# The eight column-tiled products of a modulation part issued as one group, once its four weight tiles have landed

## The chip, the core and the metric

The kernel runs on one core of a Trainium2 chip. The metric is the device time of one execution in microseconds (us). TensorE (PE) multiplies; PEld is its weight load, which overlaps the products; VectorE (DVE), ScalarE (ACT) and GpSimd (POOL) do elementwise work; SP issues most of the transfers from memory.

## What is computed

The reference is a network of four layers over 256 latent and 256 context tokens of 1024 features. Layer i mixes tokens by i % 3 (0: gated DeltaNet, 1: differential attention, 2: mLSTM), so layers 0 and 3 are DeltaNet layers; a dense squared-ReLU MLP follows. Each of the two sub-layers is modulated by vectors that come from the conditioning, six per layer and stream:

```
m_lat = jnp.split((s_lat @ w_mod[i] + b_mod[i])[:, None, :], 6, axis=-1)
m_ctx = jnp.split(s_ctx @ w_mod[i] + b_mod[i], 6, axis=-1)
hl = modulate(xl, m_lat[0], m_lat[1])          # x * (1 + scale) + shift
...
xl = layer_norm(ALPHA * xl + m_lat[2] * yl, ln_g[i, 0], ln_b[i, 0])
xl = layer_norm(ALPHA * xl + m_lat[5] * sq_relu_mlp(modulate(xl, m_lat[3], m_lat[4]), w1[i], w2[i]), ...)
```

`w_mod[i]` is 1024 by 6144. Only two rows are multiplied by it (context and latent conditioning), so the weights are the moving operand and the two rows the stationary one.

## The kernel before

Dense products (`dense`, lines 165 to 175; `passes`, line 218) take blocks of 128 output features. A weight block is loaded by SP (`load`, line 143), split into two parts of reduced width by ACT (`whi`, line 161) and DVE (`wlo`, line 162), and multiplied in three passes by eight k-tiles: 24 products of 128 by 512.

The modulation of a layer is cut into 12 parts of 512 columns. A part has four weight tiles of 512 KB (tag `wm`, four buffers, `WM`, so one part fills them all), each with two k-tiles side by side. `mod_chunk` (line 353) multiplies a part: for each of its four tiles, two products whose stationary operand is 128 by 32 (`sil`, a window that puts the two conditioning rows at one of four pairs of columns). Each product writes to 32 of the 128 partitions of one PSUM bank (`tile_position`), so tile g uses column groups 0 and 1 of the array where g is even, 2 and 3 where it is odd. In the trace one product is two instructions: a tile is 4, a part is 16. Four parts gather in one bank (`modps`); then ACT copies it (`modsb`, line 369) and `mod_cols` (line 372) turns it into columns.

The first four parts of layer 0 belong to `proj_start` (line 224), where the order on PE is written out by hand. The other 44 wait in `self.todo` (layer 0 has four parts of its own vectors first, the order is by layer and part). `fill` (line 678) takes the next: it asks for its four tiles on the SP queue and calls `mod_chunk`. The mixers call it between dense blocks, at places that constants give: `MODS` for the DeltaNet layers (line 43), `AM` for attention, `MM` for mLSTM; `run` (line 646) does what is left over at the end of a mixer. So layer 0 does 20 parts, the layers after it 8 each.

The order in the code is not yet the order on the engines. The program is built in a Tile context with `schedule_with_timeline_sim=True`: a planner simulates the engines and transfers and issues on each engine what its simulation has ready, earlier code first; `high_priority(offset=n)` moves what stands in its block ahead, `issue_after(i)` lets it come after instruction i on that engine, and a manual dependency adds an edge, with a semaphore (`Sync`) or for the order alone (`NoSync`). A tile of a pool waits until one of the tag's buffers is free. On the chip every engine runs the planned order; an instruction that waits holds up what is behind it on its engine or queue.

Before the change the eight products of a part are bound to nothing but their own tile, so the planner issues each tile's pair as soon as it reckons that tile to be there, and puts other products in between.

Of the kernel before, what the change touches and what calls it, by code (L numbers as in the profile page):

```python
# [17 lines left out]
P = 128  # L18
# [22 lines left out]
MODTAG = "oos"  # L41
AHEAD = 1
# [31 lines left out]
# columns of the packed per-partition parameters  # L74
# [7 lines left out]
# columns of the packed shape-only constants  # L82
# [8 lines left out]
# diagonal blocks of the triangular inverse: (partition quarter, half, direction, block)  # L91
# [20 lines left out]
class Net:  # L112
# [52 lines left out]
    def dense(self, w, act, ps, streams=BOTH):  # L165
        """ps[out feature, token] = sum over the eight k-tiles, in three exact float32r passes"""
# [3 lines left out]
        for k in range(8):  # L170
# [4 lines left out]
            nc.tensor.matmul(ps[:, c], lo[:, s], rh[:, c], start=False, stop=k == 7)  # L175
# [7 lines left out]
    def heads(self, kind, j):  # L183
        """the first blocks of a mixer"""
# [3 lines left out]
    def prepare_first(self, srcs, early=WHL):  # L188
        """blocks of the next stage, in parts while the norm before it runs"""
        self.ahead = [self.wblock(s, keep=i >= early, tag=AW) for i, s in enumerate(srcs)]  # L190

    def proj_first(self, srcs, act, streams=BOTH):
        """blocks at the start of a stage: their context halves, then their latent halves, k-tile by k-tile"""
# [24 lines left out]
    def passes(self, w, act, ps, k, c):  # L218
        """one k-tile's part of a block's product"""
        for i, (lhs, rhs) in enumerate(((w[0], act[k][0]), (w[0], act[k][1]), (w[1], act[k][0]))):  # L220
            self.nc.tensor.matmul(ps[:, c], lhs[:, c128(k)], rhs[:, c], start=k == 0 and i == 0, stop=k == 7 and i == 2)  # L221
            yield

    def proj_start(self, srcs, act):
        """the first blocks of all, as their operand comes in by quarters (q): M its modulation, C the operand, U a block's part"""
# [53 lines left out]
    def new_act(self, nm, n=8):  # L279
        """k-tiles of an operand as (hi, lo)"""  # L280
# [6 lines left out]
    def new_h(self):  # L287
        """k-tiles of a sub-layer's operand as (hi, lo), then the same in pairs"""
# [4 lines left out]
    def setup(self):  # L293
# [9 lines left out]
        # a window of 32 columns puts the two streams at any of the first four pairs of columns  # L303
# [18 lines left out]
        # the normalized rows come as -2 n  # L322
# [7 lines left out]
        self.mod = {}  # L330
        self.hn = 0
# [7 lines left out]
    def later(self, n, f, *a):  # L339
        """emit f(*a) after n further blocks"""  # L340
# [12 lines left out]
    def mod_chunk(self, li, q, u, n, ws, gs=range(4)):  # L353
# [1385 lines left out]
```

## Time and profile before

| what | value |
|---|---|
| runs | 2792.53, 2791.49, 2788.17 us, median 2791.49 |
| profiled execution | span 2787.1 us from the first to the last instruction; its time outside the span is not listed |
| PE | 2648.8 us busy (95%) |
| PEld | 2121.4 us (76%) |
| DVE | 1569.6 us (56%) |
| ACT | 1282.5 us (46%) |
| transfers | 379.75 MB, mean 136 GB/s |

Times of the trace are us from the start of the span. Busy is the union of an engine's instructions. An instruction of PE is drawn with a modelled end, so two neighbours can overlap. "Idle before" is the time in which the engine had nothing to do just before the instruction, with what released it.

### The profile page before, as it was taken

Reading aid. Unit: us, or ns where it says so; the run is one execution under the profiler, and the core shown is the slowest. Engines: PE = TensorE matmul, PEld = TensorE weight load, DVE = VectorE, ACT = ScalarE, POOL = GpSimd, SP = SyncE. Lnnn points to the kernel's source line nnn. Section 1 sums busy time; section 2 is a strip of 40 time slices with the busy share of each in tenths; the row PEclk is TensorE's granted clock in tenths of the full one; section 3 lists DMA queues with packets and bytes.
Section 4 is the critical chain, followed back from the end, with each engine's and each line's share of the span. In section 5 each row is a group of like instructions: output and inputs, shape, how many; then the busy total and the mean of one; then the engine's idle time right before and its main releaser. Section 6 shows DMA issues by size and latency. Waiting matters only on the chain. (4 is left out here: it accounts for less than half of the span.)

```text
span 2787.1 us, 40628 instructions
## 1 busy us (share of the span) xinstructions
PE 2648.8 (95%) x15984; PEld 2121.4 (76%) x15984; DVE 1569.6 (56%) x3353; ACT 1282.5 (46%) x2504; POOL 105.2 (4%) x172
## 2 busy tenths in 40 slices
PE   8999999999999999899999999999999998988998
PEld 4766578888888655888888876688888886678997
DVE  4688756533347455653334644563333679877555
ACT  4545376533344344353334434452333465546554
POOL 0111011000000000000000000000000011011000
PEclk9999999999999999999999999999999989889999
DMA  7587754132232334313233234423232246534353
GB/s 306 187 290 251 249 165 154 46 99 93 97 117 84 107 127 159 106 53 99 91 98 120 82 127 173 171 70 98 91 98 91 91 149 242 187 114 137 121 184 127
DMA packets 105982, 379.75 MB, mean 136 GB/s; under 512 B 12120, under 2 KB 14168, under 8 KB 105792
## 3 DMA queue, kind: packets, MB, share of 16 engines
q1 hardware_dynamic: 91808, 328.24, 34.7%
q0 software_dynamic: 13696, 48.06, 5.2%
q8 instruction: 125, 2.05, 0.3%
q10 hardware_dynamic: 288, 0.87, 0.1%
q14 instruction: 65, 0.53, 0.1%
HBM read 353.97 MB, written 23.15 MB: 135 GB/s over the span
## 5 line engine op out<-in xcount | busy, mean ns | idle before, releaser
L161 ACT CAST whi<-raw 128x1024 fp32r<-128x1024 f32 x360 | 377.3, 1049 | 845.7 <-PE psd L174 781.2
L162 DVE TENSOR_TENSOR wlo<-raw,whi 128x1024 fp32r<-128x1024 f32 x360 | 440.5, 1224 | 425.7 <-ACT whi L161 423.7
L173 PE MATMUL psd<-hh,whi 128*128 128x512 f32 (+1 forms) x1552 | 581.9, 375 | 4.2 <-ACT whi L161 4.1
L175 PE MATMUL psd<-hh,wlo 128*128 128x512 f32 (+1 forms) x1552 | 579.1, 373 | 0.7 <-DVE wlo L162 0.5
L174 PE MATMUL psd<-hl,whi 128*128 128x512 f32 (+1 forms) x1552 | 579.2, 373 | 0.0
L173 PEld LDWEIGHTS psd<-hh,whi 128*128 128x128 f32 x1552 | 293.5, 189 | 82.4 <-issue 19.1
L175 PEld LDWEIGHTS psd<-hh,wlo 128*128 128x128 f32 x1552 | 293.4, 189 | 71.6 <-issue 17.1
L174 PEld LDWEIGHTS psd<-hl,whi 128*128 128x128 f32 x1552 | 293.7, 189 | 65.6 <-issue 16.3
L173 PE MATMUL psd<-u,whi 128*128 128x512 f32 (+1 forms) x928 | 337.4, 364 | 1.2 <-ACT whi L161 1.2
L175 PE MATMUL psd<-u,wlo 128*128 128x512 f32 (+1 forms) x928 | 337.6, 364 | 0.1
L174 PE MATMUL psd<-u,whi 128*128 128x512 f32 (+1 forms) x928 | 337.5, 364 | 0.0
L546 DVE SCALAR_TENSOR_TENSOR xa<-psd,mod,xa 128x256 f32<-128x256 f32 x280 | 126.5, 480 | 306.9 <-PE psd L175 276.1
L173 PEld LDWEIGHTS psd<-u,whi 128*128 128x128 f32 x928 | 175.2, 189 | 31.4 <-ACT whi L161 1.6
L174 PEld LDWEIGHTS psd<-u,whi 128*128 128x128 f32 x928 | 175.1, 189 | 30.1
L175 PEld LDWEIGHTS psd<-u,wlo 128*128 128x128 f32 x928 | 175.2, 189 | 29.9 <-DVE wlo L162 0.3
L364 PE MATMUL modps<-wm,sil 128*32 128x512 f32 x768 | 167.0, 627 | 14.0 <-DVE sil L306 7.0
L277 DVE TENSOR_TENSOR u<-relu,u 128x512 fp32r<-128x512 f32 (+1 forms) x128 | 79.7, 625 | 64.8 <-ACT u L276 64.8
L788 DVE SCALAR_TENSOR_TENSOR kq<-conv,convh,kq 128x508 f32<-128x508 f32 (+3 forms) x128 | 85.5, 687 | 2.6 <-ACT kq L781 2.2
L364 PEld LDWEIGHTS modps<-wm,sil 128*32 128x32 f32 x768 | 25.9, 110 | 74.8 <-issue 46.8
L221 PE MATMUL psd<-hh,khi 128*128 128x256 f32 (+1 forms) x248 | 73.3, 303 | 3.5 <-ACT hh L430 3.5
L221 PE MATMUL psd<-hl,khi 128*128 128x256 f32 (+1 forms) x248 | 76.2, 308 | 0.1
L629 ACT ACTIVATE relu<-relu 128x512 f32<-128x512 f32 (+1 forms) x128 | 73.4, 579 | 3.6
(390 smaller groups left out, 4359.3 us busy)
## 6 DMA issues: line engine op xcount, KB each, us to landing
raw<-in_w_dram SPq DMA_DIRECT2D x256, 512.0 KB, 3.5
wm<-in_w_mod_dram SPq DMA_DIRECT2D x192, 512.0 KB, 5.4
raw<-in_w_in_a_dram SPq DMA_DIRECT2D x61, 512.0 KB, 4.9
raw<-in_w_qkog_c_dram SPq DMA_DIRECT2D x17, 512.0 KB, 4.7
row<-gcd POOLq DMA_DIRECT2D x16, 512.0 KB, 5.0
raw<-in_w_out_a_dram SPq DMA_DIRECT2D x16, 512.0 KB, 4.3
raw<-in_w_qk_b_dram SPq DMA_DIRECT2D x16, 512.0 KB, 4.3
ed<-row SPq DMA_DIRECT2D x12, 512.0 KB, 3.8
```

The source lines that it names most:

```text
L161: nc.scalar.copy(hi, raw)
L162: nc.vector.tensor_tensor(out=lo, in0=raw, in1=hi.bitcast(F32), op=ALU.subtract)
L173: nc.tensor.matmul(ps[:, c], hi[:, s], rh[:, c], start=k == 0, stop=False)
L174: nc.tensor.matmul(ps[:, c], hi[:, s], rl[:, c], start=False, stop=False)
L175: nc.tensor.matmul(ps[:, c], lo[:, s], rh[:, c], start=False, stop=k == 7)
L221: self.nc.tensor.matmul(ps[:, c], lhs[:, c128(k)], rhs[:, c], start=k == 0 and i == 0, stop=k == 7 and i == 2)
L277: self.nc.vector.tensor_tensor(out=lo, in0=src, in1=hi.bitcast(F32), op=ALU.subtract)
L364: nc.tensor.matmul(self.mps[r:r + 32, :], self.sil[:, 2 * g + i, 6 - 2 * u:38 - 2 * u], ws[g][:, 512 * i:512 * i + 512], start=u == 0 and ...
L546: i = getattr(self.nc.vector, name)(**k).ins
L629: nc.scalar.activation(r, r, AF.Square)
L788: nc.vector.scalar_tensor_tensor(out=y3[:, :, o], in0=x3[:, :, i], scalar=tap(t), in1=y3[:, :, o], op0=ALU.mult, op1=ALU.add)
```

## The change

`mod_chunk` gets the list of its tiles' loads. The first of its eight products then depends on all four loads, and each further one follows the one before it in issue order. `fill` puts the group behind the last dense product that was written before it (`self.mm`, kept by `dense` and `passes`) and gives it a priority of 1000 (`MPRI`). The loads move to `fetch_mod`: those of the next part are asked for right behind the group of the part before, except behind the last part of a layer's share (`QUOTA`), where the next `fill` asks for its own. Comments were removed, too.

```diff
+MPRI = 1000
+QUOTA = 20, 8, 8, 8
...
-            nc.tensor.matmul(ps[:, c], lo[:, s], rh[:, c], start=False, stop=k == 7)
+            self.mm = nc.tensor.matmul(ps[:, c], lo[:, s], rh[:, c], start=False, stop=k == 7).ins
...
+    def depend(self, i, on, wait=False):
+        self.tc.add_manual_dep(i, on.name, mybir.DependencyInfo(mybir.DependencyClass.Sync if wait else mybir.DependencyClass.NoSync,
+                                                                mybir.DependencyReason.DATA), reason="depend")
-    def mod_chunk(self, li, q, u, n, ws, gs=range(4)):
+    def mod_chunk(self, li, q, u, n, ws, gs=range(4), loads=()):
...
+        for l in loads:
+            self.depend(mm[0], l, True)
+        for a, b in zip(mm, mm[1:]) if loads else ():
+            self.depend(b, a)
...
+            self.quota = QUOTA[n]
...
-        for li, q in self.todo[:n]:
+        for _ in range(min(n, len(self.todo))):
             self.tick()
-            ws = []
-            for g in range(4):
-                ws.append(self.wp.tile([P, 1024], F32, tag="wm", name="wm", bufs=WM))
-                self.load(ws[-1], self.ins["w_mod"][li, q, g])
-            sb = self.mod_chunk(li, q, q % 4, 4, ws)
+            self.fetch_mod()
+            li, q = self.todo.pop(0)
+            ws, loads = self.fetched
+            self.fetched = None
+            with self.tc.issue_after(self.mm), self.tc.high_priority(offset=MPRI):
+                sb = self.mod_chunk(li, q, q % 4, 4, ws, loads=loads)
...
-        self.todo = self.todo[n:]
+            self.quota -= 1
+            if self.quota:
+                self.fetch_mod()
+
+    def fetch_mod(self):
+        if self.fetched is None and self.todo:
+            l, q = self.todo[0]
+            ws = [self.wp.tile([P, 1024], F32, tag="wm", name="wm", bufs=WM) for _ in range(4)]
+            self.fetched = ws, [self.load(w, self.ins["w_mod"][l, q, g]) for g, w in enumerate(ws)]
```

## Rows read from the trace of the kernel before

**Rows 1.** Page, busy us (share of the span) and instructions of two engines.
```profile
PE 2648.8 (95%) x15984; PEld 2121.4 (76%) x15984; DVE 1569.6 (56%) x3353; ACT 1282.5 (46%) x2504; POOL 105.2 (4%) x172
```

**Rows 2.** Page, costliest groups: count, busy us, mean ns, idle before and its releaser.
```profile
L364 PE MATMUL modps<-wm,sil 128*32 128x512 f32 x768 | 167.0, 627 | 14.0 <-DVE sil L306 7.0
```

**Rows 3.** Timeline of PE, 164.8 to 167.2 us: start, us, instruction, count.
```profile
165.01 0.39 PE L174 MATMUL psd<-hl,whi 128*128 128x512 f32 x1
165.24 0.39 PE L175 MATMUL psd<-hh,wlo 128*128 128x512 f32 x1
165.56 1.05 PE L364 MATMUL modps<-wm,sil 128*32 128x512 f32 x4
166.54 0.50 PE L173 MATMUL psd<-hh,whi 128*128 128x512 f32 x1
```

**Rows 4.** Timeline of PE, 252 to 256 us.
```profile
252.92 1.92 PE L364 MATMUL modps<-wm,sil 128*32 128x512 f32 x16
254.78 0.50 PE L173 MATMUL psd<-hh,whi 128*128 128x512 f32 x1
255.11 0.40 PE L174 MATMUL psd<-hl,whi 128*128 128x512 f32 x1
```

**Rows 5.** Timeline of PE, first and last piece of the 117 after the start.
```profile
54.87 1.90 PE L364 MATMUL modps<-wm,sil 128*32 128x512 f32 x10
...
2430.18 1.05 PE L364 MATMUL modps<-wm,sil 128*32 128x512 f32 x4
```

**Rows 6.** Five stages, line 364 alone: PE busy us (instructions), granted clock, DMA share, GB/s.
```profile
54.00:331.00 277.00, 54.46 (x256) 1.00 0.70 244
331.00:375.00 44.00, 17.10 (x64) 0.88 0.72 250
923.00:1094.00 171.00, 26.60 (x128) 1.00 0.41 141
1623.00:1778.00 155.00, 25.88 (x128) 1.00 0.49 175
2300.00:2432.00 132.00, 25.48 (x128) 0.92 0.62 215
```

**Rows 7.** The same stages, all work: PE, PEld, DVE, ACT, POOL busy, granted clock, DMA.
```profile
54.00:331.00 277.00, 270.04 (x1744) 182.60 (x1742) 220.79 (x513) 135.84 (x264) 27.31 (x42) 1.00 0.70 244
331.00:375.00 44.00, 35.29 (x582) 19.00 (x582) 17.84 (x31) 16.73 (x42) 1.83 (x4) 0.88 0.72 250
923.00:1094.00 171.00, 168.60 (x763) 103.72 (x762) 85.93 (x227) 70.47 (x190) 0.00 (x0) 1.00 0.41 141
1623.00:1778.00 155.00, 155.00 (x688) 105.46 (x686) 74.96 (x242) 64.86 (x154) 3.98 (x6) 1.00 0.49 175
2300.00:2432.00 132.00, 114.45 (x1051) 80.67 (x1051) 116.69 (x279) 75.10 (x156) 10.52 (x13) 0.92 0.62 215
```

**Rows 8.** Loads of `wm` issued from 1676.9 to 1678.6 us, one part.
```profile
L146 SPq DMA_DIRECT2D wm<-in_w_mod_dram x4: 328/401/422, 1676.9 to 1678.3; - x4
...
DMA to landing us min/median/max: 3.5/5.2/6.6
```

**Rows 9.** Timeline of PE, first and last products of that part.
```profile
1683.90 1.05 PE L364 MATMUL modps<-wm,sil 128*32 128x512 f32 x4
...
1693.96 1.05 PE L364 MATMUL modps<-wm,sil 128*32 128x512 f32 x4
```

**Rows 10.** Timeline of PE, 362 to 372 us, with the idle time before in brackets.
```profile
367.33 1.92 PE L364 MATMUL modps<-wm,sil 128*32 128x512 f32 x4 [2.30 <-DMA wm<-in_w_mod_dram]
```

**Rows 11.** Line 364 on PE from 54 to 375 us: idle before, us and times.
```profile
  DMA wm<-in_w_mod_dram: 3.2, 2
```

**Rows 12.** Waits of the SP queue: us in total, times, longest.
```profile
SPq L146 <- PE modps L364: 334.0, 100, 15.7
```

**Rows 13.** Waits of all engines, longest total: us, times, longest.
```profile
ACT whi L161 <- PE psd L174: 781.2, 278, 11.1
```

More of the change, by code (lines that the diff above doesn't have):

```diff
@@ L220, in passes @@
         for i, (lhs, rhs) in enumerate(((w[0], act[k][0]), (w[0], act[k][1]), (w[1], act[k][0]))):
-            self.nc.tensor.matmul(ps[:, c], lhs[:, c128(k)], rhs[:, c], start=k == 0 and i == 0, stop=k == 7 and i == 2)
+            self.mm = self.nc.tensor.matmul(ps[:, c], lhs[:, c128(k)], rhs[:, c], start=k == 0 and i == 0, stop=k == 7 and i == 2).ins
             yield
@@ L359, in mod_chunk @@
             self.mps = self.ps("modps", self.mod_tag)
+        mm = []
         for g in gs:
@@ L363, in mod_chunk @@
                 r = 32 * (2 * (g % 2) + i)
-                nc.tensor.matmul(self.mps[r:r + 32, :], self.sil[:, 2 * g + i, 6 - 2 * u:38 - 2 * u],
-                                 ws[g][:, 512 * i:512 * i + 512], start=u == 0 and g < 2, stop=u == n - 1 and g >= 2,
-                                 tile_position=(0, r))
+                mm.append(nc.tensor.matmul(self.mps[r:r + 32, :], self.sil[:, 2 * g + i, 6 - 2 * u:38 - 2 * u],
+                                           ws[g][:, 512 * i:512 * i + 512], start=u == 0 and g < 2, stop=u == n - 1 and g >= 2,
+                                           tile_position=(0, r)).ins)
+        for l in loads:
+            self.depend(mm[0], l, True)
+        for a, b in zip(mm, mm[1:]) if loads else ():
+            self.depend(b, a)
         if u == n - 1 and gs[-1] == 3:
@@ L678, in fill @@
     def fill(self, n=1):
-        for li, q in self.todo[:n]:
+        for _ in range(min(n, len(self.todo))):
             self.tick()
-            ws = []
-            for g in range(4):
-                ws.append(self.wp.tile([P, 1024], F32, tag="wm", name="wm", bufs=WM))
-                self.load(ws[-1], self.ins["w_mod"][li, q, g])
-            sb = self.mod_chunk(li, q, q % 4, 4, ws)
+            self.fetch_mod()
+            li, q = self.todo.pop(0)
+            ws, loads = self.fetched
+            self.fetched = None
+            with self.tc.issue_after(self.mm), self.tc.high_priority(offset=MPRI):
+                sb = self.mod_chunk(li, q, q % 4, 4, ws, loads=loads)
             if q % 4 == 3:
                 self.later(1, self.mod_cols, li, sb, range(q - 3, q + 1))
-        self.todo = self.todo[n:]
+            self.quota -= 1
[6 more added lines that the diff above has]
+            self.fetched = ws, [self.load(w, self.ins["w_mod"][l, q, g]) for g, w in enumerate(ws)]
     def weave(self, n, dense, *gens):
```

## The prediction, made before the change was run

> **What bounds the kernel now.** I read the page's busy times first. TensorE (PE) is busy for 95% of the span, VectorE (DVE) for 56% [rows 1]: in the whole, time taken off PE should come off the span. A busy share is a mean, though, so I then asked which PE work the change touches. The modulation products (`modps`, line 364) hold PE for 167.0 us [rows 2]. These are 192 weight tiles of four instructions each; 16 of the tiles belong to the start, which the change leaves alone, so 176 tiles, or 44 parts, remain.
>
> The timeline of PE then shows why these products cost what they do. In a stream of dense products one starts every 0.23 us, although each is drawn 0.39 us long. A modulation tile on its own (four instructions, two of the four column groups of the array) is drawn 1.05 us, keeps the next product away for 0.98 us, and starts 0.32 us after its forerunner instead of 0.23 [rows 3]. When all four tiles of a part stand together, sixteen instructions are drawn 1.92 us, the next product starts 1.86 us after the first of them, and is itself followed after 0.33 us instead of 0.23 [rows 4]. So four tiles apart cost 3.92 us between starts and four together 1.86. Between the first and the last piece after the start [rows 5] I counted 117 unbroken pieces in the timeline for the 44 parts; the rest of the working is what happens when they become 44.
>
> Last I cut the span into the stages in which the pieces lie, first with line 364 alone [rows 6], then with every engine [rows 7]. The reader is to see that the five stages differ: PE is full in the first, third and fourth; in the second and fifth it stands idle for 9 of 44 and 18 of 132 us, while DVE is busy for 117 of the 132.
>
> **The change, part by part.**
>
> *Eight products together.* No instruction is added or removed on PE; the pieces merge. From the stage table, minus parts times 1.92: 54.46 - 16 x 1.92 = 23.7; 17.10 - 4 x 1.92 = 9.4; 26.60 - 8 x 1.92 = 11.2; 25.88 - 15.36 = 10.5; 25.48 - 15.36 = 10.1 [rows 4, 6]. Sum 65.0 us. The seams come on top. One seam costs 0.09 us before the piece, gives 0.07 back where the next product starts before the drawn end, and costs 0.10 behind: 0.12 us [rows 3, 4]. The stages hold 46, 11, 20, 20 and 20 pieces, so 30, 7, 12, 12 and 12 seams go: 3.6, 0.8, 1.4, 1.4, 1.4. Together PE gets free for 27.3, 10.3, 12.7, 12.0 and 11.6 us: 73.9 us.
>
> *How much of that reaches the end.* This is where I choose. In the third and fourth stage PE is idle for 2.4 and 0 us and DVE is at half, so nothing else is near: I take 90% and 95%, 11.4 and 11.4. In the first stage PE is full, but DVE is busy for 220.8 of 277 us, which becomes 88% of the shorter stage: convolutions, splits and the triangular inverse will sometimes be late next. I take three quarters, 20.5. In the second stage PE already has gaps that the pieces partly fill: half, 5. In the fifth DVE is as busy as PE and the inverse sets the pace of the middle: 45%, 5.2 [rows 7]. Sum 53.5 us. The bounds of this term are 0 and 73.9.
>
> *The wait.* The first product of a part now waits for four transfers, where each tile's first product waited for its own; behind it on PE stand all dense products and transposes, and for those wait the evacuations on ScalarE (ACT) and DVE. The four tiles of one part, asked for back to back, landed 3.5 to 6.6 us after their issue [rows 8]. The planner used the first of them at 1683.90 and the last at 1693.96, 9.1 us after the last landing (1678.3 + 6.6) [rows 8, 9]: it reckons loads later than they come, so a group put after the last one has cover. Against that stands the end of the first layer, where products waited 2.30 us for their tile [rows 10]. Bounds: a gain of 3.2 us, all that PE waited for modulation tiles in the first two stages [rows 11], and a loss of 44 x 3.1 us = 136 us if PE stands each time from the first landing to the fourth. I take 0, since of the two rows the first is that of a part with dense work around it, as nearly all are.
>
> What a wait costs beyond itself: after the 2.30 us the four instructions took 1.92 us and not 1.05 [rows 10], half speed, and the stage's granted clock was 0.88 [rows 7]. The Trainium skill, page "TensorE: Matmul & The Clock Gate", Part 1, says that the throttled state is the default and that activity releases it. The row agrees. By the rule each wait would also double the group behind it, 1.92 us more, 44 x 1.92 = 84 us on top of the loss bound; by the rows of the dense stages, which kept a clock of 1.00, nothing is added.
>
> *The loads move.* They are asked for one part ahead. On the SP queue each part issues the same four loads; the queue stood 334.0 us waiting for modulation products to release their buffers, and the weight blocks' loads go through the same queue [rows 12]. Before, a buffer was refilled as its own tile was done; now four come free within 1.9 us and refill in a burst. A part's cycle becomes at least 1.9 + 6.6 = 8.5 us. The first stage has 277/16 = 17 us for a part, the second 44/4 = 11, the others 16 to 21. So only the second can run late, and its cover is the recurrence, which leaves PE idle there; without this cover up to a few us per part would show, which is in my half. Of the POOL queue nothing is moved. The weight blocks are covered as well: ACT's casts wait for PE 781.2 us in all, not for loads [rows 13].
>
> *Priority.* The group and ACT's copy of the bank go ahead of other ready work: each pushes others back by 1.9 us on PE, work that must be done anyway. Cost 0, by PE being in order and full; the upper bound is one group before each step of a chain, in the fifth stage 8 x 1.9 = 15 us, which is in the 45%.
>
> **Sum.** The profiled span is 2787.1 us, the median of the runs 2791.5, 4.4 more. 2787.1 - 53.5 = 2733.6 for such a span, **2738 us** for the median.
>
> **The rivals.**
>
> *All of it pays.* DVE's 88% is still under PE's share, so the first and fifth stage may shrink in full and the 3.2 us of waits go too: 2791.5 - 73.9 - 3.2 = 2714. Against it: the idle PE in the second and fifth stage.
>
> *Other engines take over in the two DeltaNet layers.* If the chains of DVE and ACT set the first, second and fifth stage, only 11.4 + 11.4 us remain: 2768. For it: DVE's 117 of 132 us in the fifth. Against: no idle PE in the first. The Trainium skill, page "Trainium Kernel Development and Optimization", Performance Expectations, holds matmul busy time to be a bad metric and the weight loads' busy share a good one. That share is 66% in the first stage (182.6 of 277), so by the rule PE is less full there than its row says. The 0.23 us between starts under 0.39 us drawn agree that drawn times overlap, and this is why I cost by starts.
>
> *The wait for four takes the place of the pieces: slower.* If the planner's loads are early against the chip's in the new order, PE stands in front of each group with everything queued behind. It decides from a mean stand of 73.9/44 = 1.7 us per part; with 3.1 us each it is 2791.5 - 73.9 + 136 = 2854. For it: the 2.30 us. Against: the 9 us of cover.
>
> *It does not do what it says.* The order is planned anew, and other products could still get between the eight, or the planner could have to hold groups back for a bank: 2791.
>
> **How the numbers follow.** Chances: forecast 0.50 (2725 to 2755), all of it 0.17, other engines 0.20, the wait 0.09, nothing 0.04. A measurement of this kernel tells about 0.2% (5.6 us) from no change. Faster by more than that are the first three: 0.87; within it the last: 0.04; slower: 0.09. The range runs from 2713, the full price, to 2776, which takes in the case of the other engines with some us of new planning noise; the wait, the nothing and a little of the spread stay outside.
>
> **What would show it.** Right: 44 pieces of sixteen in PE's timeline after the start, each some 1.92 us; line 364 busy for 167 - 65 = 102 us; PE's idle time nearly unchanged in the third and fourth stage, each 11 us shorter; DVE's share in the first near 88%. Wrong: pieces of four still there; an idle time of PE ended by the modulation's loads above some 20 us; the stages to the end of each mixer unchanged with more idle PE, ended by DVE; a granted clock below 1.00 in the first stage.

## The result, and the profile after

The changed kernel takes **2750.53 us** (median of four runs, 2748.84 to 2754.96), the kernel before beside it 2789.83: a ratio of 0.986 with a 95% interval of 0.9847 to 0.9873, 39.3 us less. The forecast was 2738: the direction and the main cause held, and the time came out 12.5 us above it. Two further sets of runs of the same order of instructions gave 0.9866 (0.9846 to 0.9887) and 0.9871 (0.9854 to 0.9888), 34 to 37 us against the runs beside them, so the effect is some 34 to 39 us.

First the page of the changed kernel: busy time per engine, then the group of the modulation products with its count, busy us, mean ns, and idle time before them.

```profile
PE 2589.6 (94%) x15984; PEld 2126.0 (77%) x15984; DVE 1567.0 (57%) x3353; ACT 1282.2 (47%) x2504; POOL 103.3 (4%) x172
...
L373 PE MATMUL modps<-wm,sil 128*32 128x512 f32 x768 | 106.7, 640 | 23.1 <-DMA wm<-in_w_mod_dram 15.8
```

Beside [rows 1, 2]: the instructions are as many as before, the modulation products hold PE 60.3 us less (167.0 to 106.7), PE as a whole 59.2 less (2648.8 to 2589.6). The span went from 2787.1 to 2748.4, by 38.7. The difference, 20.5 us, is new idle time of PE: 138.3 before, 158.8 after (span less busy). So the saving on PE came in nearly full, and a third of it came back as idle time. The rest of this part is where.

The timeline of PE in the changed kernel shows what the pieces became, the first group after the start and then some with their waits (start, us, instruction, count, idle before in brackets):

```profile
61.94 1.92 PE L373 MATMUL modps<-wm,sil 128*32 128x512 f32 x16
...
206.15 3.10 PE L373 MATMUL modps<-wm,sil 128*32 128x512 f32 x16 [2.02 <-DMA wm<-in_w_mod_dram]
...
323.45 3.27 PE L373 MATMUL modps<-wm,sil 128*32 128x512 f32 x16 [2.31 <-DMA wm<-in_w_mod_dram]
...
334.79 3.64 PE L373 MATMUL modps<-wm,sil 128*32 128x512 f32 x16 [5.27 <-DMA wm<-in_w_mod_dram]
...
345.76 1.92 PE L373 MATMUL modps<-wm,sil 128*32 128x512 f32 x16 [1.08 <-DMA wm<-in_w_mod_dram]
```

All 44 parts are one piece of sixteen now, 1.92 us each where the clock is full. Only seven of them waited for a load, for 0.52 to 5.27 us and four of the seven between 311 and 346 us, near the end of layer 0; three of the seven then ran slow (3.10, 3.27 and 3.64 us).

The waits of the whole execution say the same (engine, line, what it waited for: us, times, longest):

```profile
PE q L898 <- DVE T L876: 17.0, 3, 13.5
PE modps L373 <- DMA wm<-in_w_mod_dram: 15.8, 12, 5.3
```

Before, these two waits came to 11.5 us (longest 9.6) and 6.9 us. The loads cost PE 8.9 us more, and a wait for DVE, in the triangular inverse, 5.5.

Now the stages, all engines, as in [rows 7]: PE, PEld, DVE, ACT, POOL busy, granted clock, DMA share, GB/s. The stages moved, so the ends are set anew, near those of the same work (the fourth and fifth windows hold more instructions than before): layer 0 up to the recurrence, its recurrence, attention, mLSTM, layer 3.

```profile
54.00:310.00 256.00, 248.91 (x1758) 185.59 (x1756) 219.30 (x512) 136.41 (x265) 26.24 (x41) 0.99 0.74 264
310.00:352.00 42.00, 25.13 (x553) 14.64 (x551) 18.20 (x31) 12.70 (x29) 2.13 (x4) 0.80 0.69 244
...
900.00:1060.00 160.00, 157.70 (x766) 104.78 (x765) 83.72 (x224) 69.65 (x188) 0.00 (x0) 0.99 0.43 153
1580.00:1746.00 166.00, 161.53 (x764) 120.11 (x763) 81.69 (x257) 71.12 (x165) 6.22 (x10) 0.98 0.48 174
2249.00:2389.00 140.00, 112.74 (x1093) 86.87 (x1091) 118.19 (x285) 81.16 (x167) 12.91 (x19) 0.89 0.57 198
```

In the first stage PE is as full as before and DVE's share rose from 80% to 86% (219.30 of 256). In the second PE's busy time fell from 35.29 of 44 us to 25.13 of 42, with 29 instructions fewer in the window. In the last, PE is busy for 81%, 87% before.

To compare stages more closely I cut the span by dense products in every kernel, counting those that write `psd` in order of start (products 0, 780, 850, 3000, 3600, 5700, 6300, 8550 and 9100). Other work can still fall on the other side of a cut: in e1, 168 more instructions of PE stand before the cut between layer 0's blocks and its recurrence than before the change, in e2 16 and in e8 8 fewer, so of these three only the sum of the two columns compares. In us, with the names of the runs below; "rest" is the other stretches between the first dense product and the last, idle is span less PE busy, half is the time at 1.2 GHz in the clock's record:

| kernel | layer 0 blocks | layer 0 recurrence | attention | mLSTM | layer 3 mixer | rest | idle | half | pieces |
|---|---|---|---|---|---|---|---|---|---|
| before | 304.7 | 130.4 | 270.4 | 230.1 | 266.8 | 1544.4 | 138 | 128 | 117 |
| after | 281.3 | 134.3 | 259.9 | 220.2 | 273.8 | 1538.6 | 159 | 162 | 44 |
| e13, the same again | 284.0 | 133.8 | 259.5 | 218.1 | 270.1 | 1540.6 | 161 | 155 | 44 |
| e4, without order edges | 288.2 | 133.6 | 260.1 | 219.6 | 276.5 | 1539.5 | 163 | 179 | 44 |
| e1, no wait for four | 304.7 | 120.1 | 267.4 | 230.7 | 271.4 | 1541.0 | 135 | 138 | 109 |
| e2, group alone | 282.2 | 137.0 | 267.3 | 225.2 | 267.5 | 1539.0 | 152 | 144 | 65 |
| e3, no priority | 286.1 | 128.7 | 267.2 | 222.8 | 268.9 | 1540.8 | 146 | 155 | 62 |
| e6, layer 3 as before | 282.9 | 132.2 | 260.0 | 218.7 | 271.1 | 1540.6 | 157 | 149 | 52 |
| e7, layer 3 no priority | 288.9 | 133.6 | 260.2 | 218.5 | 267.1 | 1543.6 | 166 | 148 | 45 |
| e8, even places | 290.3 | 138.0 | 257.5 | 219.2 | 273.7 | 1539.6 | 168 | 169 | 44 |
| e9, tail in pieces | 288.6 | 134.1 | 257.0 | 219.8 | 267.9 | 1541.5 | 153 | 145 | 55 |
| e10, pairs | 285.8 | 128.9 | 258.0 | 224.0 | 268.9 | 1539.6 | 155 | 149 | 69 |
| e11, layers 1 and 2 only | 304.9 | 125.0 | 257.5 | 219.6 | 276.8 | 1539.1 | 145 | 117 | 88 |
| e12, best of each | 282.6 | 128.4 | 259.7 | 218.3 | 268.7 | 1543.1 | 155 | 145 | 50 |

In the changed kernel the first, third and fourth stage gain 23.4, 10.5 and 9.9 us, the two others **lose** 3.9 and 7.0. The rest, whose order on PE is the same in all fourteen, varies by 5.8 us, so a sum of stages is not known better than that. The kernel before has the longest rest and the changed kernel the shortest: 5.8 of the 38.7 us between these two executions are such scatter.

### The profile page after: what moved, and what is told of

It is laid out like the page before. It is cut to its first block, busy times and chain, and to the rows that moved or that the text cites. A ratio compares the mean times of both kernels' runs of the same rounds, so it can differ in the third digit from the quotient of the medians.

```text
span 2748.4 us, 40698 instructions
## 1 busy us (share of the span) xinstructions
PE 2589.6 (94%) x15984; PEld 2126.0 (77%) x15984; DVE 1567.0 (57%) x3353; ACT 1282.2 (47%) x2504; POOL 103.3 (4%) x172
## 4 chain that ended last, share of the span: by engine, by line
PE 77%; DVE 10%; ACT 6%; issue 2%; DMA 2%; POOL 0%; SPq 0%; ACTq 0%; DVEq 0%; POOLq 0%
PE psd L177 18%; PE psd L175 18%; PE psd L176 18%; PE psd L223 7%; PE modps L373 2%; DVE xa L560 2%; PE num L1561 1%; PE sp L1331 1%; DMA wm<-in_w_mod_dram 1%; PE psd L1299 1%; PE psd L1297 1%; PE psd L1298 1%; PE ops L1127 1%; PE op L1360 1%; ACT row L970 1%
## 5 line engine op out<-in xcount | busy, mean ns | idle before, releaser
L373 PE MATMUL modps<-wm,sil 128*32 128x512 f32 x768 | 106.7, 640 | 23.1 <-DMA wm<-in_w_mod_dram 15.8
L813 DVE SCALAR_TENSOR_TENSOR kq<-conv,convh,kq 128x510 f32<-128x510 f32 (+3 forms) x128 | 85.7, 689 | 10.8 <-ACT kq L806 10.5
```

The source lines that it names most:

```text
L373: mm.append(nc.tensor.matmul(self.mps[r:r + 32, :], self.sil[:, 2 * g + i, 6 - 2 * u:38 - 2 * u], ws[g][:, 512 * i:512 * i + 512], start=u ...
L813: nc.vector.scalar_tensor_tensor(out=y3[:, :, o], in0=x3[:, :, i], scalar=tap(t), in1=y3[:, :, o], op0=ALU.mult, op1=ALU.add)
```

## Experiments

Each kernel is the changed kernel with the edit shown, except where it says otherwise. Ratios are to runs of the kernel before on the same chip, with 95% intervals.

**e1: does the wait for four make the groups, or do the earlier loads, the place and the priority?** The loads list, and with it the wait and the order edges, is left out.

```diff
-                sb = self.mod_chunk(li, q, q % 4, 4, ws, loads=loads)
+                sb = self.mod_chunk(li, q, q % 4, 4, ws)
```

> The changed kernel without the wait for four loads and without the order among the eight products; loads one part ahead, the place behind the last dense product and the priority of 1000 stay. If the gain of 39 us comes from merging the pieces, the pieces are back (some 110 or more after the start, modulation products drawn busy for about 167 us) and the time is near the kernel before: 2780 to 2795 us. If it comes from the early loads and the priority, the time stays near the changed kernel: 2745 to 2760 us.

Measured: 2777.25 us, ratio 0.9954 (0.9939 to 0.9968). Of the 44 parts 20 stood whole, the rest were nearly all single tiles. The page's row of the group:

```profile
L373 PE MATMUL modps<-wm,sil 128*32 128x512 f32 x768 | 152.0, 621 | 10.8 <-DVE sil L308 7.0
```

The products hold PE 15.0 us less than before, and the time is about that much shorter (0.46% of 2790 is 13), 3 us below the range expected for the pieces. Without the wait and the edges the planner still puts other work between the tiles; e4 below shows which of the two makes the groups.

**e2: the group alone.** The wait and the order edges stay; loads are asked for where they were before the change, with no place and no priority.

```diff
-            with self.tc.issue_after(self.mm), self.tc.high_priority(offset=MPRI):
-                sb = self.mod_chunk(li, q, q % 4, 4, ws, loads=loads)
+            sb = self.mod_chunk(li, q, q % 4, 4, ws, loads=loads)
...
-            self.quota -= 1
-            if self.quota:
-                self.fetch_mod()
```

> The kernel before with the wait for four loads and the order among the eight products alone: loads asked for where they were, no place behind a dense product, no priority. If merging the pieces is the cause, there are 44 to 60 pieces and most of the gain is there: 2745 to 2765 us. If the group needs priority and early loads to stay together or to have its loads in time, other products get between or PE waits: 2775 to 2800 us.

Measured: 2764.22 us, 0.9899 (0.9884 to 0.9914). 65 pieces, the products hold PE 124.5 us: 42.5 less than before, of which 28 arrive (1.01% of 2790). That is between the two expectations: more pieces than forecast for the first, and most of the gain. The order edges do not keep other products out from between the eight; they only fix their order among themselves.

**e3: no priority.** Loads a part ahead and the place behind a dense product stay.

```diff
-            with self.tc.issue_after(self.mm), self.tc.high_priority(offset=MPRI):
+            with self.tc.issue_after(self.mm):
```

> The changed kernel without the priority of 1000; groups, wait, place behind the last dense product and early loads stay. With the group alone (no early loads, no place, no priority) 65 pieces were left and the gain was 27 of 39 us. If the priority is what keeps other products out, again some 60 pieces and 2758 to 2768 us. If the early loads and the place made the difference, 44 to 50 pieces and 2745 to 2755.

Measured: 2754.34 us, 0.9865 (0.9851 to 0.988): not told apart from the changed kernel, with the pieces of the first expectation (62, and 121.3 us of modulation products) and the time of the second. In the table, without priority, layer 0's blocks, attention and mLSTM are 4.8, 7.3 and 2.6 us longer than in the changed kernel, and the recurrence of layer 0 and layer 3 5.6 and 4.9 shorter; the differences of the blocks and of layer 3 are no larger than what one order shows from execution to execution (281.3 to 288.2 and 270.1 to 276.5 in the changed kernel, e13 and e4). The shorter recurrence came back in e12, whose PE order in layer 0 is the same as here: 128.4.

**e4: wait and priority without order edges.**

```diff
-        for a, b in zip(mm, mm[1:]) if loads else ():
-            self.depend(b, a)
```

> The changed kernel without the edges among the eight products; the wait for four loads stays on the first product alone, so the other seven may go as soon as their own tile is there. If the wait is what makes the group only together with the order, the other products run ahead in pieces: 80 or more pieces and 2770 to 2790 us. If the first product's wait and the priority alone bring them together, 44 to 50 pieces and within 4 us of 2750.

Measured: 2755.82 us, 0.9871 (0.9854 to 0.9888), 44 groups; the time is 1.8 us outside the 4 that were expected. The order in the trace is the same on all engines as in the changed kernel, apart from 32 by 32 products that run side by side on PE: the edges decide nothing. With e1 this leaves the wait for four as what makes the groups, and with e2 and e3 the priority as what keeps them whole. That makes e4 a second execution of one order, and e13 below a third.

**e6: layer 3 issues its parts as before the change** (no group, no loads ahead, no place, no priority there; `self.n` is the layer's index).

```diff
+            if self.n == 3:
+                sb = self.mod_chunk(li, q, q % 4, 4, ws)
+            else:
+                with self.tc.issue_after(self.mm), self.tc.high_priority(offset=MPRI):
+                    sb = self.mod_chunk(li, q, q % 4, 4, ws, loads=loads)
...
-            if self.quota:
+            if self.quota and self.n < 3:
```

> The changed kernel with layer 3 as before the change (pieces, no priority, loads asked for in place). Layer 3 lost 6 us in the changed kernel against its own start. If the groups and their priority hold up the chain of the inverse on VectorE there, the 6 us come back: 2742 to 2747 us. If the loss is one of the new plan and of half-clock stretches there, not of the groups, the time stays within 3 us of 2750 or gets longer.

Measured: 2748.03 us, 0.9846 (0.9828 to 0.9863). Layer 3 takes 271.1 us with eight more pieces and 5.2 us more of modulation products on PE than in the changed kernel, where the three executions took 270.1 to 276.5. Giving PE that work back cost nothing in layer 3, and the time stayed within the 3 us that were expected if groups and priority are not what holds layer 3 up.

**e7: layer 3 keeps the group and the loads ahead, but neither place nor priority.**

```diff
+            if self.n == 3:
+                sb = self.mod_chunk(li, q, q % 4, 4, ws, loads=loads)
+            else:
+                with self.tc.issue_after(self.mm), self.tc.high_priority(offset=MPRI):
+                    sb = self.mod_chunk(li, q, q % 4, 4, ws, loads=loads)
```

> The changed kernel with the groups of layer 3 kept together but without the place behind the last dense product and without priority. Layer 3 from its first block to the end of its recurrence took 266.8 us before, 273.8 in the changed kernel, 267.5 with groups alone and 271.1 with its old form. If the priority holds up the chain of the inverse, it comes to 265 to 269 us and the time to 2741 to 2746. If it is the new plan and the half clock, it stays at 271 to 275 and the time within 3 us of 2750.

Measured: 2754.24 us, 0.9861 (0.9844 to 0.9878). Layer 3 takes 267.1 us, as expected if priority holds it up, and no less than before. Nothing was gained in all: in this execution layer 0's blocks took 7.6 us more and the rest 5.0, although the order on PE in both is that of the changed kernel; the section on the hardware returns to that.

**e8: the parts of layer 0 spread evenly,** so that four instead of seven of the first 19 come in the last seven blocks, near where the loads were late.

```diff
-MODS = ((0, 2, 3, 4, 7, 8, 10, 12, 13, 14, 16, 20, 22, 23, 24, 25, 26, 27, 28), (8, 11, 12, 14, 16, 20, 21, 22, 24, 28))
+MODS = ((0, 2, 3, 5, 6, 8, 9, 11, 12, 14, 15, 17, 18, 20, 21, 23, 24, 26, 27), (8, 11, 12, 14, 16, 20, 21, 22, 24, 28))
```

> The changed kernel with the 19 places of layer 0 spread evenly over the 29 blocks instead of seven in the last seven. In the changed kernel PE stood 12 us in layer 0 for modulation loads, 9 of them at its last four parts, and the clock fell behind them. If these stands cost what they take plus the half clock, the waits of PE for these loads fall from 15.8 to under 9 us in all and the time by 8 to 14 us: 2736 to 2743 us. If at that place PE would have stood for the inverse anyway, the waits go and the time stays within 4 us of 2750.

Measured: 2756.49 us, 0.9872 (0.9855 to 0.9888). The waits of PE in front of the products (us, times, longest) fell from 15.8 us for the loads to this:

```profile
PE modps L373 <- DMA wm<-in_w_mod_dram: 6.4, 5, 3.1
PE modps L373 <- issue: 5.7, 3, 3.5
```

Yet layer 0 took 428.3 us (290.3 + 138.0) against 415.6 in the changed kernel, and against 417.8 and 421.8 in the other two executions of its order. The waits fell as expected, but neither expected time came. This does not clear the loads: the chain of work that ended last still goes through loads of `wm` here, of 7.5 and 7.1 us, and through two stands of PE for which the profile shows no releaser, 2.6 us before a group and 5.0 before a product of the inverse.

**e9: the four parts that layer 0 issues last for layer 1 in single tiles, each waiting for its own load.**

```diff
-                sb = self.mod_chunk(li, q, q % 4, 4, ws, loads=loads)
+                sb = self.mod_chunk(li, q, q % 4, 4, ws, loads=() if li == 1 and q >= 8 else loads)
```

> The changed kernel with the last four parts of layer 0 (layer 1, parts 8 to 11) in pieces again: no wait for four loads and no order among the eight for these alone. In the changed kernel PE stood 9.4 us for modulation loads around the recurrence of layer 0 and that stage took 134.3 us; in the kernel with all parts in pieces it took 120.1 with 0.7 us of such stands. If the wait for four costs there what is missing, the stands fall under 3 us, the stage comes to 120 to 128 us and the time to 2736 to 2745. If the recurrence sets the stage whatever the products do, the time stays within 4 us of 2750.

Measured: 2749.72 us, 0.9848 (0.9831 to 0.9864). There are 11 more pieces, and the waits of PE for the loads (us, times, longest) halve:

```profile
PE modps L373 <- DMA wm<-in_w_mod_dram: 8.0, 9, 2.2
```

Its stage takes 134.1 us against 134.3, 133.8 and 133.6. Idle time ended by the loads there fell from 9.4 to 4.0 us, and the products held PE 17.8 us instead of 10.8; the time did not move. Two things changed in opposite directions, so this does not show that either is free, and the chain that ended last still goes through loads here (8.6 and 4.3 us), then along single tiles between the inverse's products. The 120.1 us of e1, on which the expectation rests, is a stage with other work in it, as said at the table.

**e10: two groups of eight, each waiting for its own two tiles.**

```diff
-        for l in loads:
-            self.depend(mm[0], l, True)
-        for a, b in zip(mm, mm[1:]) if loads else ():
-            self.depend(b, a)
+        for i, l in enumerate(loads):
+            self.depend(mm[i // 2 * 4], l, True)
+        for i in (0, 1, 2, 4, 5, 6) if loads else ():
+            self.depend(mm[i + 1], mm[i])
```

> As the changed kernel, but a part is two groups of eight instructions, each waiting for its own two tiles (the two tiles of a pair use different column groups). Theory (what counts is that tiles on different column groups stand side by side): in the kernel before a piece of eight took 1.00 us between starts, so two pairs cost 2.00 and, where they come apart, one more seam of 0.12, against 1.86 for sixteen: at most 44 x 0.26 = 11 us more PE work than the changed kernel, less where the planner leaves pairs side by side, and the waits for loads fall below the changed kernel's 15.8 us, to 5 to 10: 2745 to 2758 us. Rival (all four tiles have to be together, a pair is no cheaper than two single tiles): 44 x 2.06 = 91 us of PE work come back and the time is that of the kernel before or above, 2785 or more.

Measured: 2746.71 us, 0.9846 (0.9827 to 0.9864). 19 parts stood whole, 25 came as two pairs. The timeline of PE shows one of each kind:

```profile
63.42 1.92 PE L373 MATMUL modps<-wm,sil 128*32 128x512 f32 x16
65.27 0.50 PE L175 MATMUL psd<-hh,whi 128*128 128x512 f32 x1
...
99.69 1.07 PE L373 MATMUL modps<-wm,sil 128*32 128x512 f32 x8
100.69 0.41 PE L778 MATMUL gcp<-gg,cons 128*128 128x32 f32 x2
```

A pair keeps the next product away for 1.00 us, a single tile for 0.98 [rows 3]: the second tile of a pair, on the other two column groups, is nearly free. The group of four is two such pairs in a row, 1.86. The Trainium skill, page "TensorE: Matmul & The Clock Gate", the table under "Why this matters for your kernels", says that small products whose outputs lie in distinct 32-partition groups run concurrently, with 2.38 times the rate for three of them; here two tiles of two column groups each gave 1.96 times (2 x 0.98 / 1.00), so the row agrees. The rival, that all four are needed, is out. One expectation missed: the waits for loads came to 13.6 us and not to 5 to 10.

**e11: the change in layers 1 and 2 only.** Layers 0 and 3 issue as before.

```diff
+            if self.n in (0, 3):
+                sb = self.mod_chunk(li, q, q % 4, 4, ws)
+            else:
+                with self.tc.issue_after(self.mm), self.tc.high_priority(offset=MPRI):
+                    sb = self.mod_chunk(li, q, q % 4, 4, ws, loads=loads)
...
-            if self.quota:
+            if self.quota and self.n in (1, 2):
```

> The changed form in layers 1 and 2 alone; layers 0 and 3 issue their parts as before the change. Theory (the stages add up, and what was given back in idle time and half clock belongs to the two DeltaNet layers): attention 10.5 us and mLSTM 9.9 us shorter as in the changed kernel, the other stages as in the kernel before: 2790 - 20 = 2770 us, idle PE time near 138 us as before. Rival (what is saved in layers 1 and 2 is given back elsewhere too, or the DeltaNet layers' plans move although their code does not): 2776 or more, or stages of layers 0 and 3 off by more than 3 us.

Measured: 2772.11 us, 0.9937 (0.9915 to 0.996), 18.4 us less than before, where 20 was expected (2764.62 to 2776.01; the profiled execution is the fastest of the four). Attention and mLSTM give 12.9 and 10.5. The idle time, 145.2 us, is nearer to that of before (138.3) than to that of after (158.8), as expected. But the rival has a point: layer 0's recurrence came out 5.4 us shorter with the order of before on PE, and layer 3, in its old form though planned anew, 10.0 us longer. So these two stages vary by some 5 to 10 us without the groups.

**e12: best of each.** Layer 0 without priority as in e3, layers 1 and 2 as in the changed kernel, layer 3 as in e7.

```diff
+            if self.n == 3:
+                sb = self.mod_chunk(li, q, q % 4, 4, ws, loads=loads)
+            elif self.n == 0:
+                with self.tc.issue_after(self.mm):
+                    sb = self.mod_chunk(li, q, q % 4, 4, ws, loads=loads)
+            else:
+                with self.tc.issue_after(self.mm), self.tc.high_priority(offset=MPRI):
+                    sb = self.mod_chunk(li, q, q % 4, 4, ws, loads=loads)
```

> Groups with the wait for four everywhere; layer 0 with loads a part ahead and place but no priority, layers 1 and 2 as in the changed kernel, layer 3 without priority, place behind a dense product. Theory (stages add up: layer 0 as in the run without any priority, 414.8 us against 415.6; layer 3 as in the run without priority there, 267.1 against 273.8): 2750.5 - 7.5 = 2743 us. Rival (layer 0 and layer 3 are planned anew with each edit, and their stages scatter by some 10 us whatever the edit was for): anywhere from 2743 to 2758, with layer 0's stages off by more than 5 us from 414.8.

Measured: 2745.82 us (2742.67 to 2749.11), 0.9839 (0.9822 to 0.9855). It is the lowest of all, 44.6 us below the kernel before, and 2.8 above what the sum of stages gave; layer 0 took 411.0 us and layer 3 268.7, where 414.8 and 267.1 were expected. Its interval overlaps that of the changed kernel and those of e6, e9 and e10, so "best" is likely here, not shown.

**e13: the changed kernel once more,** with no edit.

> The changed kernel, nothing edited, to see whether its own stages come back. Theory (a stage's time and its stretches at half clock belong to the order on the engines): layer 0 to the end of its dense blocks 281 us again, its tail 134, layer 3 in all 274, half clock in all near 161 us, each within 2 us; time 2750. Rival (the clock falls by chance, from execution to execution): one of the stages off by 3.4 us or more, in steps of the half-clock stretches.

Measured: 2753.71 us (2748.6 to 2758.51), 0.9866 (0.9846 to 0.9887). Layer 0 took 284.0 and 133.8, layer 3 270.1, half clock in all 155 us. Attention and the recurrence of layer 0 come back within 0.5 us; layer 0's blocks, mLSTM and layer 3 are off by 2.7, 2.1 and 3.7. So the theory (each within 2 us) falls for layer 0's blocks, for layer 3 and for the half-clock time, and the rival holds: some of it changes from execution to execution.

## Why the prediction was right, and where it was off

**The price of a group: right.** 44 pieces, 1.92 us each; 65.0 us of drawn time were forecast, 60.3 came. The 4.7 us between are the groups that ran slow: the parts in [rows 4] took 1.92, the three shown above 3.10, 3.27 and 3.64, 4.25 more in sum. The price of sixteen, 1.86 us between starts, held wherever the clock was full. Over the kernels the gain follows the time taken off the products, with something lost each time and with scatter: 15.0 off gave about 13, 23.6 gave 18, 42.5 gave 28, 45.7 gave 38 and 60.3 gave 39 (e1, e11, e2, e3 and the change, each by its ratio); the others, with 53 to 60 off, gave 36 to 45.

**Attention and mLSTM: right.** 11.4 and 11.4 were forecast, 10.5 and 9.9 came, and with the change in these two alone (e11) it was 12.9 and 10.5. PE was full there and DVE at half; such a stage returned 82% or more of the 12.7 and 12.0 us that PE freed.

**Layer 0's blocks: the size right, the cause half right.** 20.5 was forecast, 23.4 came in the profiled execution. Over the six executions with this order of PE there (after, e13, e4, e6, e7, e9) it was 281.3 to 288.9 against 304.7 and 304.9 with the order of before: 16 to 24 us of the 27.3 that were to be freed on PE. I named DVE as what would be late next, the inverse included. Up to the inverse's first product PE stood for little, and nearly all arrived: from the first dense product it came 206.0 and 204.7 us with the order of before, 186.1 to 188.0 us with the new one. In the inverse PE then waits longer for DVE at one place, the product that follows the first batch of 32 by 32. In PE's timeline, the kernel before:

```profile
233.47 1.16 PE L960 MATMUL kk<-kq 128*128 128x128 f32 x8 [1.37 <-DVE bn L966]
```

The changed kernel:

```profile
216.18 1.36 PE L985 MATMUL kk<-kq 128*128 128x128 f32 x8 [1.98 <-DVE bn L991]
```

The same order once more, e4:

```profile
217.72 2.08 PE L983 MATMUL kk<-kq 128*128 128x128 f32 x8 [3.34 <-DVE bn L989]
```

The wait is 1.37 us in the old order (1.34 in e11) and 1.98 to 4.37 in the six executions of the new one. This can be a part of the quarter that I took off, but not in the changed kernel itself: PE's idle time in the whole stage was 7.5 us before and 7.6 after (9.6 to 12.4 in the other five), and what is missing from the 27.3 lies in PE's busy time, which fell by 23.5. A lower clock goes with it, which the prediction listed as a sign against itself; it is told in the section on the hardware.

**Layer 0's recurrence: wrong.** The step was "PE already has gaps that the pieces partly fill: half, 5", together with "its cover is the recurrence, which leaves PE idle there" for the loads. The stage gave nothing and lost 3.9 us (130.4 to 134.3): PE's busy time in it fell by 5.2 us, its idle time rose by 9.0, and 6.2 of these are waits for the modulation's loads (3.2 before, 9.4 after). The chain of work that ended last in the changed kernel shows that they are on the path and not beside it (start, us, what; pieces under 1 us left out):

```profile
301.77 1.92 PE modps L373 x16
304.16 6.67 DMA wm<-in_w_mod_dram
310.97 1.98 PE modps L373 x16
313.43 9.93 DMA wm<-in_w_mod_dram
323.45 3.27 PE modps L373 x16
327.60 7.05 DMA wm<-in_w_mod_dram
334.79 3.64 PE modps L373 x16
338.43 1.05 PE ktp L1216 x4
339.48 1.30 PE q L922 x32
```

The four buffers hold one part, so the loads of a part go out when the group before it is done, and they land 6.7 to 9.9 us later. The groups start 9.2 to 12.5 us apart, where the prediction reckoned with 8.5 at the least and had 11 for each part, from loads that it had read in the fourth stage. No recurrence covers this, because the inverse's own products stand behind the groups on PE: the last of them end at 347.9 us, right behind the last group, and 91.8 us later the stage is over (90.8 to 91.9 in the four other executions of this order). The time that grouping frees on PE does not shorten such a cycle of load and group.

The runs without priority fit this: in e3 and e12 the inverse's products are through before the last two groups, and the stage took 128.7 and 128.4 us. So the prediction's "priority: cost 0", with an upper bound of one group ahead of each step of a chain, was too low here, by some 5 us. Priority alone does not decide it, though: e10 keeps it, its last part was done 34.8 us into the stage and not 42.2, and the stage took 128.9. With the order of before it took 130.4 and 125.0. No run gave the modulation more buffers than one part fills, which would test the cycle by itself; what it costs in all stays open.

**Layer 3: wrong, and the profile had said why.** The step was a share of 45% of 11.6 us. The share was nothing: 266.8 us before, 270.1 to 276.5 after, and no other execution in any form (old, grouped, with priority or without, thirteen in all) took less than 267.1. The mechanism is the one that I had as a rival, "other engines take over" (for this layer DVE), and it can be read at the first product of the inverse. PE's timeline of the kernel before:

```profile
2368.81 0.28 PE L873 MATMUL q<-T,bn 32*32 32x32 f32 x2 [9.57 <-DVE T L851]
```

That of the changed kernel:

```profile
2326.83 0.28 PE L898 MATMUL q<-T,bn 32*32 32x32 f32 x2 [13.55 <-DVE T L876]
```

And the stretch from the layer's first dense product to this one, as one window (columns as in [rows 7]), in the kernel before:

```profile
2276.60:2368.80 92.20, 75.13 (x459) 60.65 (x459) 79.89 (x196) 54.41 (x119) 18.80 (x27) 0.89 0.65 228
```

And in the changed kernel:

```profile
2232.90:2326.80 93.90, 70.62 (x460) 58.02 (x459) 79.84 (x197) 53.36 (x115) 18.01 (x27) 0.89 0.66 231
```

PE does 4.5 us less, DVE the same 79.9, and the inverse starts 92.2 us after the layer's first product before and 93.9 after; PE waits 4.0 us longer in front of it. In the other kernels this stretch took 91.1 to 97.5 us. DVE's timeline shows what it waits for, the last steps of the changed kernel's chain:

```profile
2317.67 0.19 DVE L862 TENSOR_TENSOR W<-W,invt 128x31 f32<-128x31 f32 x1
2317.90 1.25 DVE L866 STREAM_TRANSPOSE R<-W 128x1024 f32<-128x1024 f32 x1
2319.07 1.86 DVE L867 STREAM_TRANSPOSE R<-W 128x1024 f32<-128x1024 f32 x1
2320.96 0.58 DVE L878 COPY T<-R 32x512 f32<-32x512 f32 x1
2321.55 1.54 DVE L876 COPY T<-R 32x512 f32<-32x512 f32 x2
2323.10 2.97 DVE L883 COPY bn<-R 32x256 f32<-32x256 f32 x8
2326.10 1.19 DVE L876 COPY T<-R 32x512 f32<-32x512 f32 x2
```

They follow one another without a gap. From the inverse's first step on DVE (`invt`) to PE's first product of it, as one window in the kernel before and one in the changed kernel:

```profile
2311.60:2368.80 57.20, 47.64 (x301) 36.31 (x300) 54.29 (x138) 25.56 (x52) 6.10 (x6) 0.96 0.65 227
...
2268.70:2326.80 58.10, 44.33 (x292) 35.67 (x293) 52.81 (x136) 23.08 (x47) 4.22 (x6) 0.88 0.62 218
```

DVE is busy for 95% of it before and 91% after, so hardly anything that PE gives back can shorten it. The reading that should have been made: ask of the stage's busiest engine not its share but whether a wait for it already stands in front of PE. It did, 9.57 us, before the change. The 7 us by which the changed kernel is worse than before in layer 3 are not explained: the 266.8 is one execution, the order of the changed kernel took 270.1 to 276.5 in four (e8 has it too in this layer), e6 and e11, in the old form, took 271.1 and 276.8, and e7, grouped, 267.1. Priority was the suspect; e9 and e10 keep it and took 267.9 and 268.9, so it is not settled.

**The wait term: small in the whole, wrong at the end of layer 0.** Forecast 0 between a gain of 3.2 and a loss of 136. The waits for loads on PE rose by 8.9 us, 6.2 of them in the layer 0 recurrence, where the chain goes through them; the term was taken from a part with dense work around it, and its loads had landed in 3.5 to 6.6 us. "Only the second can run late" came true for the two longest stands, 2.31 and 5.27 us; one of 2.02 stands in the first stage. After waits of 2.02, 2.31 and 5.27 us the group ran slow, after 0.52 to 1.08 us it did not, in e4 one ran at 1.92 us after a wait of 2.04, and 37 of the 44 groups had no load to wait for. The prediction took from the Trainium skill, page "TensorE: Matmul & The Clock Gate", Part 1, that activity releases a throttled state, and made of it that every wait would also slow the group behind it; this second step is the prediction's own, and it agrees with three of these rows and not with the others.

**The sum.** Against the forecast of 53.5 us the span gave 38.7. Of the 14.8 missing, layer 3 is 12.2 and the recurrence 8.9, attention and mLSTM 2.4; layer 0's blocks gave 2.9 more than forecast, and the rest 5.8, which was not in the forecast and lies within the scatter of executions. So that the sum came within 15 us is luck in part: without the rest the stages gave 32.9. The error lies in the shares of the two stages in which PE had gaps, 50% and 45%, which should both have been 0. The rival in which other engines take over in the DeltaNet layers (2768) was true of layer 3, and not of layer 0's blocks; in the recurrence it was the loads. Of the signs named beforehand, the pieces, the products' busy time (102 forecast, 106.7 seen), the third and fourth stage and DVE's share in the first (88% forecast, 86% seen) spoke for the forecast, and the waits for loads, 15.8 us, stayed under the 20 that were named; more idle PE ended by DVE and a clock of 0.99 in the first stage spoke against it.

## What to carry to other kernels

Here a saving on the busiest engine counted in the stages in which that engine had no gap: read the share per stage, and where a gap stands, look for the wait in front of it. If the wait's owner was late before the change, the saving turns into a longer wait (4.5 us of work less, 4.0 of waiting more in layer 3). Where one group's inputs fill all the buffers, a wait for all of them makes a cycle of load and group; check whether anything that matters stands behind the group in the engine's order. Products that share no column groups of the array should be issued next to each other, and what brought this about in the planned order was a common wait on their inputs, with priority to keep them whole; waiting for two of four was enough here.

## What the runs showed of the hardware

**The same order runs at different clocks.** After, e13 and e4 have one order of instructions on every engine (but for 32 by 32 products that run side by side), and e6, e7 and e9 the same on PE in layer 0's blocks. Their time for that stage was 281.3, 284.0, 288.2, 282.9, 288.9 and 288.6 us, and the time at the lower of the two clock levels, 1.2 GHz, in it 8.4, 10.2, 21.3, 4.6, 15.4 and 22.2 us. With the order of before it was 1.6 and 3.4. The windows around the inverse show it, 50 us each. The kernel before:

```profile
215.00:265.00 50.00, 45.48 (x609) 31.62 (x609) 42.20 (x88) 32.48 (x68) 6.49 (x10) 1.00 0.73 262
```

The changed kernel:

```profile
195.00:245.00 50.00, 45.48 (x599) 32.27 (x598) 42.01 (x90) 31.25 (x67) 7.43 (x11) 0.93 0.79 281
```

And e4, the same order:

```profile
195.00:245.00 50.00, 41.96 (x522) 30.69 (x515) 40.19 (x87) 28.78 (x62) 7.18 (x11) 0.86 0.78 277
```

What PE did before the fall at the inverse is alike in all six: a stretch of 32 by 32 products, then the wait for DVE's `bn` of 1.98 to 4.37 us, and around its end the lower level begins, for 3.4 to 6.8 us. A second such stretch with 0.92 to 2.99 us of idle was followed by a second fall in e13, e4, e7 and e9, and in e6 (1.69 us) by none. There are falls elsewhere in this stage too, at 206.75 us in the changed kernel, within the group that had waited 2.02 us, and at 136 to 139 us in e13, e4 and e9. In the order of before, the waits of 1.37 and 1.34 us (e11) for `bn` were followed by no fall; later waits of 2.88 and 2.80 us by none in the kernel before and by one in e11. Behind a fall dense products take nearly twice as long: in e7 they started every 0.43 us after it and every 0.23 again later. What decides between a fall and none, these runs don't tell.

Over the whole kernel the half-clock time rose from 128 to 162 us, and at the lower level PE shows as busy for longer with the same work, so some of the saving may have come back in this way. That it costs half its length where PE is full was not tested by itself. Between two of the executions it fits: 288.2 less 281.3 is 6.9 us, for 12.9 us more at 1.2 GHz (e4 and the changed kernel). Between others it doesn't: e7 is 7.6 us longer than the changed kernel for 7.0 more.

**Loads.** The modulation's tiles landed a median of 6.3 us after their issue, 5.4 before, in bursts of four. At the end of layer 0, where a part's loads wait for the group before, the loads on the chain took 6.7 to 9.9 us. Elsewhere no stage shows a cost of it.
